# A state-space mixer and a mixture of experts on one core: row norms and weight splits ahead, the p projection moved into the router, one tile and one exponential per scan step

## The chip, the cores and the metric

The kernel runs on one core of a Trainium2 chip. The metric is the device time of one execution in microseconds (us). The engines are TensorE (PE, with its weight loads PEld), VectorE (DVE), ScalarE (ACT), GpSimd (POOL) and SyncE (SP), which here only issues transfers (DMA). Each engine works through its own queue in order and waits for others by semaphores.

## The reference

One layer on x (1024 tokens by 1024) with a side input p (1024 by 256), all float32:

```python
h = x + ssd_mixer(rms_norm(x), ...)        # in-projection, conv of 4 taps, chunked scan, out-projection
h = h + hier_moe(rms_norm(h), ...)         # 64 experts: best of 8 groups, then 2 of its 8 experts
gate = sigmoid(rms_norm(h) @ ple_w_gate + ple_b_gate)
h = h + gate * (p @ ple_w_proj)
out = rms_norm(h)
# the chunked scan, per chunk of 128 tokens and head, acum = cumsum(dt * A):
y_diag = (C B^T * tril(exp(acum[l] - acum[s]))) @ xc
y_off = C @ state * exp(acum)
state = state * exp(acum[-1]) + B^T (xc * exp(acum[-1] - acum))
```

## The kernel before

The work has three stages, one behind the other on PE.

**Scan stage (`ssd`).** The tokens are done in two halves (`hf`) of 512, and in each half four groups `g` of eight heads: eight units. For a half, `x_half` loads the rows of x to get their norms (squares on ACT or DVE, `rsqrt` on DVE), spreads the norms by four transposes on PE (line 177) into a tile along the tokens, loads the columns of x (`xT`), scales them and splits them into a high and a low part, `xh` and `xl`. A unit's `project` makes ten tiles of 128 channels: each loads 128 columns of `w_in`, splits them (`wh` on ACT, `wl` on DVE, line 70) and runs 24 matmuls (lines 204 to 206). Conv and SiLU follow on DVE and ACT. Between the ten tiles of a unit the scan of the unit before is placed by a plan of steps: `front(c)` of chunk c prepares and `back(c)` multiplies, in the order front 0, front 1, back 0, front 2, back 1, front 3, back 2, back 3. A front loads the running sums `acd` of its eight heads, broadcast over the partitions, into the tile `ac` (line 322), takes the exponential into `ec` (338), subtracts each token's own sum from `ac` in place (340), and takes the second exponential of that (342). The back's matmuls (369, 371) read both. `ac` has three buffers, which the row loads of x use too, and `ec` two. `step_sizes` writes `acd` once per half.

**Out-projection and router (`out_router`, `route`).** Eight token tiles in sets of 2, 3 and 3 go through 16 k steps (lines 505 to 507). The router's steps of a set (`stats`, `turn`, `logits`, `first`, `second`, `third`) run between the products of the next; those of the last set stand alone at the end: transposes (612), logits (618), positions (685 to 690), and two packings (714) from which the first gather of rows starts. Meanwhile `moe_weights` loads what the last stage needs.

**Expert stage (`moe`).** Eight groups of eight experts, in a manual order on PE. A group has 24 parts of 16 matmul instructions (line 1027), each on two weight tiles of 1 MB from a ring of eight (line 782). Between the parts stand other pieces: `spread` (1017), `combine` (1090, 1091), and, in the first half of a group, the gated side input of the group before (`ple`): transposes of h (898), 16 gate matmuls (908), and the projection of p: `fetch_p` gathers 128 rows of p, `turn_p` transposes them (855) and `project_p` multiplies them by `wpp` (861), whose result DVE takes from PSUM. Group 6 does two projections more, for the end (`early`).

Instructions whose place nothing fixes are put in order when the program is built, by the tile scheduler.

Of the kernel before, what the change touches and what calls it, by code (L numbers as in the profile page):

```python
# [20 lines left out]
KD = D // 128  # L21
# [20 lines left out]
class K:  # L42
# [64 lines left out]
    def ssd(self, left, right):  # L107
# [35 lines left out]
        def x_half(hf):  # L143

            ss, rs, *tmp = (wk.tile([128, HC], F32, name=n) for n in ("rs", "rs", "nt0", "nt1", "nt2"))
            cols = []

            def columns():
                for j in range(2):
                    w = wraw.tile([128, KD, 256], F32, name="w").rearrange("p a b -> p (a b)")  # L150
                    w = w.rearrange("p (k t) -> p k t", t=HT)
                    nc.sync.dma_start(w, a["xT"].rearrange("(k p) t -> p k t", p=128)[:, 4 * j:4 * j + 4,
                                                                                      hf * HT:(hf + 1) * HT])
                    cols.extend(w[:, k] for k in range(4))

            for i in range(HC):
                t = hf * HC + i
                xt = (wk.tile([128, D], F32, name="ec") if i == 3 else wk.tile([128, D], F32, name="ac", bufs=3))
                nc.sync.dma_start(xt, a["x"][t * 128:(t + 1) * 128, :])
                if i == HC - 1:  # L160
                    if hf == 0:
                        W.append(load(2 * DI, 2 * DI + 512))
                    columns()
# [14 lines left out]
            rsb = wk.tile([128, HT], F32, name="dT", bufs=1)  # L178
            nc.scalar.activation(rsb, pr.rearrange("p c t -> p (c t)"), AF.Copy)

            def scale(k):
                nc.vector.tensor_mul(cols[k], cols[k], rsb)
# [4 lines left out]
            yield  # L187
# [75 lines left out]
        def proj(w, i, x):  # L263
            wh = wsp.tile([128, KD, 128], F32R, name="wh")
            wl = wsp.tile([128, KD, 128], F32R, name="wl")
            self.split(wh, wl, w[:, :, i * 128:(i + 1) * 128])
            ps = self.ps_mm.tile([128, 512], F32, name="mm")
            mm3(ps, wh, wl, x)
            return ps

        def conv_tile(hf, w, i, x, m):
# [5 lines left out]
            ps = proj(w, i, x)  # L277
# [11 lines left out]
        def project(hf, g):  # L289
            x = X[hf]  # L290
            w = W.pop() if W else load(2 * DI + g * 128, 2 * DI + 512 + g * 128)
            xT, zT = [], zp.tile([128, 4, HT], F32, name="z")
            bT = conv_tile(hf, w, 0, x, 16 + g)
            yield
            cT = conv_tile(hf, w, 1, x, 20 + g)
            U[hf, g] = bT, cT, xT, zT
            yield
            for j in range(2):
                w = load(DI + g * 512 + j * 256)
                for i in range(2):  # L300
                    xT.append(conv_tile(hf, w, i, x, 4 * g + 2 * j + i))
                    yield
            for j in range(2):
                w = load(g * 512 + j * 256)
                for i in range(2):
                    nc.scalar.activation(zT[:, 2 * j + i], proj(w, i, x), AF.Silu)
                    yield

        def scan(hf, g):
# [6 lines left out]
            def front(c):  # L316
# [4 lines left out]
                ac = wk.tile([128, 8, Q], F32, name="ac", bufs=3)  # L321
                nc.sync.dma_start(ac, bass.AP(tensor=acd.tensor, offset=acd[8 * g:8 * g + 1, cg * Q:cg * Q + 1].offset,
# [89 lines left out]
        X, SZ, U, W = {}, {}, {}, []  # L412
        for i, _ in enumerate(x_half(0)):
            if i == 0:
                nc.sync.dma_start(gk, a["ssd_norm_kp"])
            if i == HC - 1:
                small_loads()
# [3 lines left out]
        for hf, g in units:  # L421
# [5 lines left out]
            if g == 0:  # L427
                for t in (0, 1, 7, 8):
                    at(t, next, sizes, None)
            if before:  # L430
                at(0, before[2])
                at(2, before[3])
# [5 lines left out]
            if hf == 0 and g == NG - 1:  # L438
                xg = x_half(1)
                for t in (3, 4, 5, 6, 7):  # L440
                    at(t, next, xg)
# [15 lines left out]
    def out_router(self, st, tail, after_tail):  # L457
# [18 lines left out]
        self.gdd = dp.tile([128, 8, NE], F32, name="gdd")  # L476
        macc = self.macc
# [82 lines left out]
        for f in side:  # L560
            f()
# [21 lines left out]
    def route(self, t0, hs, rp, pr_p, wr, rb, macc):  # L583
# [95 lines left out]
        def third():  # L679
# [3 lines left out]
            for i in range(n + 1):  # L683
# [5 lines left out]
                if t0:  # L689
                    nc.tensor.matmul(pa[:, i], lhsT=self.onesb, rhs=macc, start=False, stop=True)  # L690
            adj, was = tl("adj", 8)[:, 0], self.more
# [29 lines left out]
            pack(self.mid, omi)  # L721
            started = tc.issue_after(self.index(rp).ins) if t0 + n == T // 128 else nullcontext()
# [16 lines left out]
    def moe_weights(self, st):  # L739
# [3 lines left out]
        wpp = cp.tile([128, 2, D], F32, name="wpp")  # L743
# [4 lines left out]
        self.pl = (wpg, wpp, bg, fn, mgp)  # L748

        def loads():  # L750
# [6 lines left out]
            for k in range(2):  # L757
                nc.sync.dma_start(wpp[:, k], a["ple_w_proj"][k * 128:(k + 1) * 128])
                yield
# [3 lines left out]
            for _ in range(10):  # L763
# [30 lines left out]
    def moe_buffers(self, st, ring):  # L794
# [4 lines left out]
        self.p0, self.po = (hp.tile([128, PD], F32, name=f"p{i}") for i in range(2))  # L799
# [39 lines left out]
    def fetch_p(self, g):  # L839
        if g < NGR - 1:  # L840
            self.gather(self.p0, self.a["p"], g)
        if self.first_of(g + 1) or g == NGR - 1:
            self.gather(self.po, self.a["p"], NGR + SET[g])
# [8 lines left out]
    def turn_p(self, p, pT, pc_):  # L852
        pt = pc_.tile([128, 2, 128], F32, name="pc")
        for k in range(2):
            self.nc.tensor.transpose(pt[:, k], p[:, k * 128:(k + 1) * 128], self.ident)
        self.nc.scalar.activation(pT, pt, AF.Copy)

    def project_p(self, pT, hf, pc_):
        pq = pc_.tile([128, 512], F32, name="pc")
        for k in range(2):  # L860
            self.nc.tensor.matmul(pq, lhsT=pT[:, k], rhs=self.pl[1][:, k, hf * 512:hf * 512 + 512],  # L861
                                  start=(k == 0), stop=(k == 1))
        return pq

    def ple(self, h, p, store, wk, pq_, pc_, own=(), pr=None):
# [3 lines left out]
        wpg, wpp, bg, fn, mgp = self.pl  # L869
# [23 lines left out]
        def tr(k0):  # L893
# [6 lines left out]
            if k0 and pr is None:  # L900
                self.turn_p(p, new("pT", [128, 2, 128]), pc_)
# [26 lines left out]
    def moe(self, s2, ring, sa):  # L928
        nc, tc, a = self.nc, self.tc, self.a
        mgp = self.pl[4]  # L930
# [5 lines left out]
        part = {"vT": vx[:, 0:1024].rearrange("p (k t) -> p k t", k=KD), "gt": vx[:, 1024:1536],  # L936
                "pT": vx[:, 1536:1792].rearrange("p (k t) -> p k t", k=2)}
# [164 lines left out]
        def ple_of(G, i, own=part):  # L1102
# [3 lines left out]
                bounds_check=T - 1, oob_is_err=False), wk, ps1, ps2, own,  # L1106
                            None if i else G.pr)

        def project(p, o):

            self.turn_p(p, part["pT"], ps2)
            for hf in range(2):
# [346 lines left out]
```

## Time and profile before

| | us |
|---|---|
| median of 3 runs | 1950.36 (1946.88 to 1954.07) |
| the profiled execution | 1954.31 |
| its span, first to last instruction | 1952.4 |
| PE busy in the span | 1848.3 |

The page's first part gives the busy time of each engine, the second its share in 40 equal slices with the granted clock of TensorE, the third the transfers; the chain of waits follows the work back from its end, and the groups of instructions name line, tile and mean duration. The lines are those of the kernel before.

### The profile page before, as it was taken

The numbers are of one execution on the slowest core, as the hardware profiler recorded it, in microseconds if no ns is written. First come the engines' busy times: TensorE is split into PE (matmuls) and PEld (weight loads), VectorE is DVE, ScalarE is ACT, GpSimd is POOL, SyncE is SP. The second block draws the span as 40 slices with busy tenths as digits, with TensorE's granted clock in tenths as the row PEclk, the third lists the DMA queues.
The fourth block names the chain that finished last, engine by engine and source line by source line (L and its number), as shares of the span: only waits on it lengthen the run. The fifth ranks groups of instructions, "written<-read, shape, count | busy, mean of one in ns | idle before, by whom it ended". The sixth has DMA issues, their size and how long they took to land.

```text
span 1952.4 us, 23158 instructions
## 1 busy us (share of the span) xinstructions
PE 1848.3 (95%) x8702; PEld 1047.1 (54%) x8702; DVE 1031.5 (53%) x2194; ACT 749.5 (38%) x1040; POOL 182.7 (9%) x276
## 2 busy tenths in 40 slices
PE   6999997999999999979999999999999999999996
PEld 4778775777887678863343333433433334334334
DVE  5497896858988876573341514423325244143223
ACT  5476766557767533322021211312222113122223
POOL 1011110201111031021000000000000000000004
PEclk9999998999999999988999999999999999999998
DMA  7425444345442787956999999999999999998883
GB/s 220 118 75 137 115 134 127 88 97 134 110 110 53 243 294 238 346 195 254 422 421 394 401 421 385 412 412 383 420 382 404 420 373 423 404 375 325 337 322 109
DMA packets 192166, 538.39 MB, mean 276 GB/s; under 512 B 16046, under 2 KB 128688, under 8 KB 143920
## 3 DMA queue, kind: packets, MB, share of 16 engines
q1 hardware_dynamic: 177744, 514.21, 72.0%
q10 hardware_dynamic: 11008, 12.94, 2.0%
q0 software_dynamic: 3296, 9.70, 1.3%
q8 instruction: 70, 1.15, 0.2%
q14 instruction: 48, 0.39, 0.1%
HBM read 520.95 MB, written 17.69 MB: 276 GB/s over the span
## 4 chain that ended last, share of the span: by engine, by line
PE 81%; DMA 7%; DVE 7%; ACT 2%; issue 2%; POOL 1%; SPq 0%; POOLq 0%; ACTq 0%; DVEq 0%
PE pup L1027 11%; PE pgate L1027 11%; PE py L1027 10%; PE mm L206 6%; PE mm L204 6%; PE mm L205 6%; PE pq L908 6%; PE pc L1017 3%; PE mm L505 2%; PE mm L506 2%; PE mm L507 2%; DMA w<-in_w_up_dram 2%; PE pc L861 2%; DMA ac<-acd 2%; PE pc L1090 2%
## 5 line engine op out<-in xcount | busy, mean ns | idle before, releaser
L204 PE MATMUL mm<-xh,wh 128*128 128x512 f32 x640 | 265.6, 415 | 3.3 <-ACT xh L197 2.2
L206 PE MATMUL mm<-xh,wl 128*128 128x512 f32 x640 | 254.5, 400 | 8.4 <-DVE wl L70 8.3
L205 PE MATMUL mm<-xl,wh 128*128 128x512 f32 x640 | 253.9, 397 | 0.3 <-DVE xl L198 0.3
L1027 PE MATMUL pup<-w,XT 128*64 128x512 f32 x1016 | 239.1, 598 | 1.6 <-DMA w<-in_w_up_dram 1.6
L1027 PE MATMUL pgate<-w,XT 128*64 128x512 f32 x1000 | 232.7, 599 | 0.0
L1027 PE MATMUL py<-w,hT 128*64 128x512 f32 (+1 forms) x1024 | 227.1, 586 | 2.1 <-DMA w<-in_w_down_dram 2.1
L70 DVE TENSOR_TENSOR yx<-py,yx 128x512 fp32r<-128x512 f32 (+1 forms) x68 | 44.8, 659 | 234.2 <-ACT yx L69 234.2
L1027 PEld LDWEIGHTS py<-w,hT 128*64 128x64 f32 x1024 | 70.0, 137 | 146.2 <-issue 138.2
L1027 PEld LDWEIGHTS pup<-w,XT 128*64 128x64 f32 x1016 | 72.1, 136 | 141.9 <-issue 131.5
L206 PEld LDWEIGHTS mm<-xh,wl 128*128 128x128 f32 x640 | 122.6, 192 | 38.5 <-DVE wl L70 12.2
L204 PEld LDWEIGHTS mm<-xh,wh 128*128 128x128 f32 x640 | 122.9, 192 | 34.2 <-issue 4.5
L1027 PEld LDWEIGHTS pgate<-w,XT 128*64 128x64 f32 x1000 | 68.7, 137 | 134.2 <-issue 129.6
L205 PEld LDWEIGHTS mm<-xl,wh 128*128 128x128 f32 x640 | 123.0, 192 | 29.9 <-issue 4.3
L908 PE MATMUL pq<-wpg,vx 128*128 128x512 f32 x256 | 123.1, 607 | 0.0
L70 DVE TENSOR_TENSOR wl<-w,wh 128x1024 fp32r<-128x1024 f32 x80 | 97.4, 1220 | 46.4 <-ACT wh L69 46.4
L69 ACT ACTIVATE wh<-w 128x1024 fp32r<-128x1024 f32 x80 | 84.3, 1054 | 72.0 <-PE mm L205 59.4
L284 DVE SCALAR_TENSOR_TENSOR xbc<-raw,convw,xbc 128x512 f32<-128x512 f32 x144 | 109.7, 762 | 3.8 <-ACT xbc L282 2.7
L506 PE MATMUL mm<-wl,yh 128*128 128x512 f32 x256 | 99.3, 398 | 2.0 <-DVE wl L517 1.9
L505 PE MATMUL mm<-wh,yh 128*128 128x512 f32 x256 | 96.0, 402 | 4.8 <-ACT yh L69 4.6
L69 ACT ACTIVATE yx<-py 128x512 fp32r<-128x512 f32 (+1 forms) x68 | 38.9, 572 | 159.4 <-PE py L1027 159.4
L1058 ACT ACTIVATE hT<-pt 128x512 f32<-128x512 f32 x31 | 18.4, 593 | 211.5 <-PE pt L1056 211.5
L507 PE MATMUL mm<-wh,yl 128*128 128x512 f32 x256 | 98.0, 393 | 0.0
(360 smaller groups left out, 2815.6 us busy)
## 6 DMA issues: line engine op xcount, KB each, us to landing
w<-in_w_up_dram SPq DMA_DIRECT2D x127, 1024.0 KB, 9.5
w<-in_w_gate_dram SPq DMA_DIRECT2D x125, 1024.0 KB, 9.1
w<-in_w_down_dram SPq DMA_DIRECT2D x120, 1024.0 KB, 9.5
w<-in_w_in_dram SPq DMA_DIRECT2D x32, 1024.0 KB, 5.6
w<-in_w_out_dram SPq DMA_DIRECT2D x48, 512.0 KB, 5.2
ac<-acd SPq DMA_DIRECT2D x32, 512.0 KB, 9.3
w<-in_w_in_dram SPq DMA_DIRECT2D x16, 512.0 KB, 8.7
yn<-yz SPq DMA_DIRECT2D x32, 256.0 KB, 4.4
```

The lines of the kernel that those rows point to most:

```text
L69: self.nc.scalar.activation(dst_h, src, AF.Copy)
L70: self.nc.vector.tensor_sub(dst_l, src, r_(dst_h))
L204: nc.tensor.matmul(ps, lhsT=wh[:, k], rhs=x[0][:, k], start=(k == 0), stop=False)
L205: nc.tensor.matmul(ps, lhsT=wh[:, k], rhs=x[1][:, k], start=False, stop=False)
L206: nc.tensor.matmul(ps, lhsT=wl[:, k], rhs=x[0][:, k], start=False, stop=(k == KD - 1))
L284: nc.vector.scalar_tensor_tensor(o, raw[:, j:j + HT], convw[:, m, j:j + 1], o, op0=OP.mult, op1=OP.add)
L505: nc.tensor.matmul(po[i][hf], lhsT=yh[:, ts], rhs=wh[:, cs], start=(k == 0), stop=False)
L506: nc.tensor.matmul(po[i][hf], lhsT=yh[:, ts], rhs=wl[:, cs], start=False, stop=False)
L507: nc.tensor.matmul(po[i][hf], lhsT=yl[:, ts], rhs=wh[:, cs], start=False, stop=(k == 15))
L908: nc.tensor.matmul(V["pq"], lhsT=V["vT"][:, k], rhs=wpg[:, k, cs], start=(k == 0), stop=(k == KD - 1))
L1017: nc.tensor.matmul(px, lhsT=x[:, k], rhs=G.S[:, i], start=(i == 0 and x is u[i][0]), stop=(i == 1 and x is u[i][1]))
L1027: nc.tensor.matmul(ps[64 * b:64 * b + 64], lhsT=xt(k0 + k, b), rhs=w[b][:, k, cs], start=(k0 + k == 0), stop=(k0 + k == K - 1))
```

## The change

Five edits. (1) The row norms are a piece of work of their own, `norms(hf)`; those of the second half run in the first unit, and their result has a tile of its own, `rsb`. (2) The splits of `w_in` come from one generator, and each tile's split is asked for before the tile ahead of it has been finished. (3) A front's sums and differences lie in one tile `ae` with two buffers; the load goes to its first half, the subtraction writes the second, and one exponential covers both. The steps `norm` and `store` of a unit stand one step later in the plan. (4) p is handed over transposed and projected for all tokens in the router's last steps, in 16 pieces of two matmuls; the result goes to memory as `ppd`. (5) The expert stage gathers rows of `ppd` (1024 wide) in place of rows of p (256 wide), five steps later, and transposes and multiplies nothing for it.

```diff
+            pr = self.ps_tp.tile([128, HC, 128], F32, name="tp")
...
+            RB[hf] = wk.tile([128, HT], F32, name="rsb", bufs=1)
+            nc.scalar.activation(RB[hf], pr.rearrange("p c t -> p (c t)"), AF.Copy)
+            yield
...
+        def proj(x):
+
+            wh, wl = ahead.pop() if ahead else next(W)
             ps = self.ps_mm.tile([128, 512], F32, name="mm")
             mm3(ps, wh, wl, x)
+            ahead.extend(w for w in [next(W, None)] if w)
             return ps
...
-                ac = wk.tile([128, 8, Q], F32, name="ac", bufs=3)
-                nc.sync.dma_start(ac, bass.AP(tensor=acd.tensor, offset=acd[8 * g:8 * g + 1, cg * Q:cg * Q + 1].offset,
+                ae = wk.tile([128, 2, 8, Q], F32, name="ae")
+                ec, ac = ae[:, 0], ae[:, 1]
+                nc.sync.dma_start(ec, bass.AP(tensor=acd.tensor, offset=acd[8 * g:8 * g + 1, cg * Q:cg * Q + 1].offset,
...
-                ec = wk.tile([128, 8, Q], F32, name="ec")
-                nc.scalar.activation(ec, ac, AF.Exp)
                 for h in range(8):
-                    nc.vector.tensor_scalar(ac[:, h], ac[:, h], acs[:, c, 8 * g + h:8 * g + h + 1], 0.0,
+                    nc.vector.tensor_scalar(ac[:, h], ec[:, h], acs[:, c, 8 * g + h:8 * g + h + 1], 0.0,
                                             op0=OP.subtract, op1=OP.min)
-                nc.scalar.activation(ac, ac, AF.Exp)
+                nc.scalar.activation(ae, ae, AF.Exp)
...
+                if hf == 0:
+                    rows = norms(1)
+                    for t in (2, 3, 4, 5, 6):
+                        at(t, next, rows)
...
+        def project():
+
+            for t in range(T // 128):
+                pr = wp.tile([128, D], F32, name="wl")
+                for hf in range(2):
+                    cs = slice(hf * 512, hf * 512 + 512)
+                    pq = self.ps_mm.tile([128, 512], F32, name="mm")
+                    for k in range(2):
+                        nc.tensor.matmul(pq, lhsT=pT[k][:, t * 128:(t + 1) * 128], rhs=wpp[k][:, cs],
+                                         start=(k == 0), stop=(k == 1))
+                    nc.scalar.activation(pr[:, cs], pq, AF.Copy)
+                    if hf:
+                        nc.sync.dma_start(self.ppd[t * 128:(t + 1) * 128], pr)
+                    yield
...
+            for n, f in zip((6, 0, 0), side[-3:]):
+                f() if f is not side[-1] else f(lambda n: [next(pieces, None) for _ in range(n)])
+                for _ in range(n):
+                    next(pieces)
+            for _ in pieces:
+                pass
...
-            if k0 and pr is None:
-                self.turn_p(p, new("pT", [128, 2, 128]), pc_)
...
-            nc.vector.tensor_mul(gt, gt, self.project_p(V["pT"], hf, pc_) if pr is None else pr[:, cs])
+            nc.vector.tensor_mul(gt, gt, pr[:, cs])
...
-                    fill[2].append(lambda: self.gather(vx[:, 1792:], a["p"], g + 1))
-                    early = [project(vx[:, 1792:], nxt.pr), project(self.p0, cur.pr)]
...
-                    if n == 10:
+                    if n == 15:
                         self.fetch_p(g)
```

Three places in the order of the built programs follow. The first is on PE. Before, the transposes that spread the second half's norms (`tp<-ident,rs`) stand inside the group of 24 matmuls that begins the second half:

```order
L205 MATMUL mm<-xl,wh 128x512
L206 MATMUL mm<-xh,wl 128x512
L204 MATMUL mm<-xh,wh 128x512
L177 MATMUL tp<-ident,rs 128x128 x4
L205 MATMUL mm<-xl,wh 128x512
L206 MATMUL mm<-xh,wl 128x512
```

Now they stand between two tiles of the very first unit:

```order
L205 MATMUL mm<-xl,wh 128x512
L206 MATMUL mm<-xh,wl 128x512
L165 MATMUL tp<-ident,rs 128x128 x4
L204 MATMUL mm<-xh,wh 128x512
L205 MATMUL mm<-xl,wh 128x512
L206 MATMUL mm<-xh,wl 128x512
```

So the row norms of the second half, with their loads, are past long before its first matmul.

The second is on SP, behind the write of the sums `acd` in the second unit; `w` are weight tiles of `w_in`. Before:

```order
L253 DMA acd<-dT 32x512
L322 DMA ac<-acd 128x8x128 x3
L260 DMA w<-in_w_in_dram 128x8x256
L322 DMA ac<-acd 128x8x128
L260 DMA w<-in_w_in_dram 128x8x128 x2
L260 DMA w<-in_w_in_dram 128x8x256
L322 DMA ac<-acd 128x8x128 x2
```

Now:

```order
L253 DMA acd<-dT 32x512
L334 DMA ae<-acd 128x8x128 x2
L260 DMA w<-in_w_in_dram 128x8x256
L260 DMA w<-in_w_in_dram 128x8x128 x2
L334 DMA ae<-acd 128x8x128
L260 DMA w<-in_w_in_dram 128x8x256
L334 DMA ae<-acd 128x8x128
```

Two broadcasts instead of three go ahead, and from then on a broadcast and a weight load take turns.

The third is on PE, at the end of the router. Before, the logits of the last token tile (`tp<-wr,uT`) are followed at once by the positions (`tris`, `onesb`):

```order
L612 MATMUL tp<-ident,h 128x128 x8
L618 MATMUL tp<-wr,uT 128x72 x8
L688 LDWEIGHTS tris
L688 MATMUL tp<-M,tris 128x72
L690 LDWEIGHTS onesb
L690 MATMUL tp<-macc,onesb 128x72
```

Now six pieces of the projection (`mm<-w,wh`, twelve matmuls) stand between them:

```order
L660 MATMUL tp<-ident,h 128x128 x8
L666 MATMUL tp<-wr,uT 128x72 x8
L593 MATMUL mm<-w,wh 128x512 x12
L736 LDWEIGHTS tris
L736 MATMUL tp<-M,tris 128x72
L738 LDWEIGHTS onesb
L738 MATMUL tp<-macc,onesb 128x72
```

Two more pieces follow the positions, two the first packing, and the last six the second packing, ahead of the first `spread`.

## Rows read from the trace of the kernel before

**Rows 1.** The page, part 1: busy us of each engine (share of the span) and instructions.

```profile
PE 1848.3 (95%) x8702; PEld 1047.1 (54%) x8702; DVE 1031.5 (53%) x2194; ACT 749.5 (38%) x1040; POOL 182.7 (9%) x276
```

**Rows 2.** Busy time by stretch, all engines. Columns: stretch and its length, busy us of PE, PEld, DVE, ACT and POOL with the number of instructions, granted clock, busy share of the DMA engines, GB/s.

```profile
90.00:112.00 22.00, 17.19 (x73) 12.48 (x72) 15.63 (x36) 15.96 (x20) 1.78 (x5) 0.84 0.23 71
290.00:335.00 45.00, 31.48 (x150) 23.61 (x149) 28.41 (x81) 27.00 (x34) 3.03 (x4) 0.85 0.45 130
360.00:380.00 20.00, 15.31 (x79) 12.70 (x80) 18.88 (x39) 12.05 (x16) 4.12 (x7) 0.83 0.40 95
...
858.00:890.00 32.00, 17.75 (x94) 11.44 (x94) 22.87 (x87) 8.77 (x16) 9.92 (x19) 0.68 0.43 150
```

**Rows 3.** What PE waited for in the whole run (us in total, times, longest).

```profile
PE mm L206 <- DVE wl L70: 8.3, 8, 2.2
...
PE py L369 <- DVE ac L352: 3.6, 2, 3.5
...
PE py L1027 <- DMA w<-in_w_down_dram: 2.1, 2, 1.3
```

**Rows 4.** The same between 250 and 500 us.

```profile
PE tp L177 <- DVE rs L66: 7.8, 1, 7.8
```

**Rows 5.** Pieces of the chain of waits that are transfers in the scan stage (start, us, what).

```profile
80.56 12.30 DMA ac<-acd
286.85 10.97 DMA ec<-in_x_dram
309.70 9.82 DMA ac<-acd
```

**Rows 6.** The issues of the broadcast loads of the sums in the whole run (queue, count, KB each, median us from issue to landing).

```profile
ac<-acd SPq DMA_DIRECT2D x32, 512.0 KB, 9.3
```

**Rows 7.** The time to landing of all transfers that touch `acd`.

```profile
DMA to landing us min/median/max: 1.6/9.3/15.1
```

**Rows 8.** What SP's queue waited for in front of these issues (us in total, times, longest).

```profile
SPq L322 <- PE py L371: 132.1, 18, 16.9
```

**Rows 9.** Loads of ACT's function tables ahead of the two exponentials (groups of instructions: count, busy us, mean ns, idle before).

```profile
L342 ACT ACT_TABLE_LOAD x24 | 30.8, 1283 | 7.4 <-DVE ed L346 2.8 <-DMA rb<-in_b_re_dram 2.3 <-DVE ac L340 2.1
...
L338 ACT ACT_TABLE_LOAD x21 | 26.9, 1283 | 0.7 <-DMA ac<-acd 0.4
```

**Rows 10.** What DVE waited for at the subtraction in the whole run (us in total, times, longest).

```profile
DVE ac L340 <- ACT ec L338: 23.3, 7, 9.6
```

**Rows 11.** Two groups of DVE instructions, the subtraction and the low part of a split, in the whole run (duration ns, least, median, most; first and last start).

```profile
L340 DVE TENSOR_SCALAR ac<-ac,acs x256: 269/279/842, 89.1 to 676.2; 128x128 f32<-128x128 f32 x128
...
L70 DVE TENSOR_TENSOR wl<-w,wh x80: 1155/1218/1325, 12.7 to 624.4; 128x1024 fp32r<-128x1024 f32 x80
```

**Rows 12.** PE in the scan stage in order of time: the first and the last of fifteen matmuls in a row, with fourteen starts between them (start, duration us).

```profile
33.10 0.39 PE L204 MATMUL mm<-xh,wh 128*128 128x512 f32 x1
...
36.28 0.39 PE L206 MATMUL mm<-xh,wl 128*128 128x512 f32 x1
```

**Rows 13.** The projection of p on PE, all of it as one group of instructions (count, busy us, mean ns, idle before and what ended it).

```profile
L861 PE MATMUL pc<-wpp,vx 128*128 128x512 f32 x72 | 36.3, 627 | 5.0 <-ACT vx L856 2.5 <-DVE ha L1092 1.3 <-DVE hb L1092 1.3
```

**Rows 14.** One projection's pieces on PE in order of time (start, us).

```profile
1149.87 0.38 PE L855 MATMUL pc<-ident,p 128*128 128x128 f32 x2
1150.18 3.65 PE L1027 MATMUL pgate<-w,XT 128*64 128x512 f32 x16
...
1177.66 1.98 PE L861 MATMUL pc<-wpp,vx 128*128 128x512 f32 x4 [0.32 <-DVE hb L1092]
1179.57 3.65 PE L1027 MATMUL pup<-w,XT 128*64 128x512 f32 x16
```

**Rows 15.** The chain of waits at the same point (the first part of the last `down`) of groups 1, 5 and 6, that is at the start of the next group's work; between the first two lie four groups.

```profile
1120.99 3.58 PE py L1027 x16
...
1633.47 3.58 PE py L1027 x16
...
1773.72 3.58 PE py L1027 x16
```

**Rows 16.** Busy time by stretch in the expert stage, columns as in rows 2.

```profile
1100.00:1180.00 80.00, 79.03 (x332) 30.48 (x330) 24.96 (x46) 19.73 (x33) 2.03 (x2) 1.00 1.01 421
1180.00:1230.00 50.00, 50.00 (x208) 17.63 (x206) 19.73 (x40) 10.16 (x15) 2.12 (x2) 1.00 0.98 378
1230.00:1310.00 80.00, 79.03 (x332) 30.33 (x328) 25.39 (x46) 18.88 (x32) 1.28 (x2) 1.00 1.01 421
```

**Rows 17.** The issues of expert weights (count, KB each, median us to landing).

```profile
w<-in_w_up_dram SPq DMA_DIRECT2D x127, 1024.0 KB, 9.5
```

**Rows 18.** PE at the end of the router and the start of the expert stage, in order of time (in brackets the idle time before and what ended it).

```profile
862.39 2.00 PE L618 MATMUL tp<-wr,uT 128*128 128x72 f32 x16
868.82 0.22 PE L688 MATMUL tp<-M,tris 128*128 128x72 bf16 x1 [4.42 <-DVE me L664]
...
872.51 0.33 PE L714 MATMUL tp<-omi,at 128*128 128x16 bf16 x6 [2.76 <-DVE at L706]
874.27 0.70 PE L714 MATMUL tp<-oms,at 128*128 128x104 bf16 x6 [1.43 <-DVE oms L728]
879.77 1.22 PE L1017 MATMUL pc<-S,uh 128*128 128x512 f32 x2 [4.80 <-ACT uh L1003]
...
889.76 3.65 PE L1027 MATMUL pgate<-w,XT 128*64 128x512 f32 x14
```

More of the change, by code (lines that the diff above doesn't have):

```diff
@@ L141, in small_loads, with norms @@
             nc.sync.dma_start(al, bcast_rows(a["a_log"], 128, 0, NH))
-        def x_half(hf):
+        def norms(hf):
             ss, rs, *tmp = (wk.tile([128, HC], F32, name=n) for n in ("rs", "rs", "nt0", "nt1", "nt2"))
[L146 to L154, printed above, removed]
             for i in range(HC):
                 t = hf * HC + i
-                xt = (wk.tile([128, D], F32, name="ec") if i == 3 else wk.tile([128, D], F32, name="ac", bufs=3))
+                if i % 2 == 0:
+                    two = wk.tile([128, 2, D], F32, name="ae")
+                xt = two[:, i % 2]
                 nc.sync.dma_start(xt, a["x"][t * 128:(t + 1) * 128, :])
[L160 to L163, printed above, removed]
                 if hf == 0 and i % 2:
@@ L261, in load, with weights, conv_tile @@
             return w
[L263 to L266, printed above, removed]
+        def weights():
+            for hf in range(2):
+                for g in range(NG):
+                    for cols in ((2 * DI + g * 128, 2 * DI + 512 + g * 128), *((DI * a_ + g * 512 + j * 256,)
+                                                                               for a_ in (1, 0) for j in range(2))):
+                        w = load(*cols)
+                        for i in range(2):
+                            wh = wsp.tile([128, KD, 128], F32R, name="wh")
+                            wl = wsp.tile([128, KD, 128], F32R, name="wl")
+                            self.split(wh, wl, w[:, :, i * 128:(i + 1) * 128])
+                            yield wh, wl
+        W = weights()
+        ahead = []
+        def proj(x):
+            wh, wl = ahead.pop() if ahead else next(W)
             ps = self.ps_mm.tile([128, 512], F32, name="mm")
             mm3(ps, wh, wl, x)
+            ahead.extend(w for w in [next(W, None)] if w)
             return ps
[L271 removed]
+        def conv_tile(hf, x, m):
             raw = rawp.tile([128, 3 + HT], F32, name="raw")
@@ L410, in scan @@
             return front, back, norm, store
-        X, SZ, U, W = {}, {}, {}, []
-        for i, _ in enumerate(x_half(0)):
+        X, SZ, U, RB = {}, {}, {}, {}
+        first, xg = norms(0), x_half(0)
+        for i in range(HC):
+            next(first)
             if i == 0:
                 nc.sync.dma_start(gk, a["ssd_norm_kp"])
-            if i == HC - 1:
-                small_loads()
+        ahead.append(next(W))
+        next(xg)
+        small_loads()
+        next(first)
+        next(xg)
         sizes = step_sizes(0)
@@ L476, in out_router @@
         self.gdd = dp.tile([128, 8, NE], F32, name="gdd")
+        self.ppd = dp.tile([T, D], F32, name="ppd")
         macc = self.macc
@@ L762, in loads @@
             nc.sync.dma_start(fn, bcast_rows(a["final_norm"], 128, 0, D))
-            for _ in range(10):
+            for _ in range(12):
                 yield
@@ L850, in parts, with ple @@
         mm(to, lhsT=v[1][:, k], rhs=w[0], start=False, stop=(k == KD - 1))
[L852 to L865, printed above, removed]
+    def ple(self, h, pr, store, wk, pq_, pc_, own=()):
         nc = self.nc
-        wpg, wpp, bg, fn, mgp = self.pl
+        wpg, bg, fn, mgp = self.pl
         V = dict(own)
@@ L1281, in moe @@
                 if g == NGR - 2:
-                    nxt.pr, cur.pr = self.h0[(g + 2) % 3], self.ho[(SET[g] - 1) % 3]
-                    fill[2].append(lambda: self.gather(vx[:, 1792:], a["p"], g + 1))
-                    early = [project(vx[:, 1792:], nxt.pr), project(self.p0, cur.pr)]
-                    for n, x in ((17, 0), (18, 0), (20, 1), (21, 1)):
-                        fill.setdefault(n, []).append(lambda x=x: next(early[x]))
+                    nxt.pr = self.h0[(g + 2) % 3]
+                    fill.setdefault(17, []).append(lambda: self.gather(nxt.pr, self.ppd, g + 1))
                 if nxt:
```

96 lines of the change are left out of this document (49 added, 47 removed).

## The prediction

> **What bounds the kernel now.** I read the busy times first: PE works 95% of the span, ACT 38%, DVE 53% [rows 1]. So the time is PE's work plus what PE loses: idle time, and time at a lower granted clock. Second, the windows by stretch: in three places of the scan and at the router's end PE idles and the clock lies at 0.68 to 0.85 of the higher of its two levels, 2.4 GHz [rows 2]; in the expert stage it is 1.00. Third, PE's waits by releaser, for the causes: the low part `wl` of a split (8.3 us in 8 waits) and the back's tile `ac` (3.6) in the scan, expert weights for only 2.1 [rows 3], and one wait of 7.8 us for the norms of the second half [rows 4]. Fourth, the chain of waits, which turns to transfers at just these places of the scan: the broadcast of the sums (12.30 and 9.82 us) and the load of x's rows (10.97) [rows 5].
>
> All sums below are made against the profiled execution, 1954.31 us. The median of the runs is 4 us lower, and the forecast is moved by as much at the end. What a measurement of this kernel can tell from no change is 0.5%, or 10 us.
>
> **Norms of the second half ahead.** The four transposes stand inside the first group of matmuls of the second half, and PE is in order: it stops there until the rows of x have landed and the norms are out. The stretch of 45 us holds 31.48 us of PE work [rows 2]: 13.5 us idle, and 45 × 0.15 = 6.75 us by which the clock fell short. All of it gone is 20.3; the wait alone is 7.8. The transposes themselves remain, and the row loads move to the first unit, where the DMA engines were 23% busy in the stretch read [rows 2]. What is late next is the scaling and splitting of x's columns on DVE, 28.41 us busy in those 45, so not all of the gap goes. I take −17 (bounds −7.8 to −20.3).
>
> **Splits a tile ahead, backs a tile later.** This aims at the waits for `wl` and `ac`, 8.3 + 3.6 us [rows 3]. They sit in stretches such as 90 to 112 (4.8 us idle, 3.5 by the clock) and 360 to 380 (4.7 and 3.4), 16.4 together [rows 2]. A split that is asked for a tile early has a tile of PE time more, but stands in DVE's queue behind other work all the same. I take −9, three quarters of the waits, between nothing and the 16.4 of the two stretches.
>
> **One tile and one exponential.** The order of the built program holds 96 loads of ACT's function tables in place of 128: 32 × 1.283 = 41 us of ACT [rows 9]. ACT is off the path, so I count nothing for it by itself. DVE's wait of 23.3 us for the first exponential [rows 10] goes too; DVE now waits for the transfer itself. What is new is that the tile has two buffers for three: the broadcasts of chunks 2 and 3 can go out only when the backs 0 and 1 have read theirs. SP waited for backs before as well, 132.1 us in 18 waits [rows 8], but with one chunk more of lead. The matmuls come every (36.28 − 33.10) / 14 = 0.227 us [rows 12], a tile of 24 takes 5.5. After a back come two tiles, 11.0 us, with the transposes of a front, and then the next back, an estimated 4 us: 15 in all until PE needs the split that stands behind the subtractions on DVE. A broadcast lands after 9.3 us at the median [rows 6], the eight subtractions take 8 × 0.28 and the split 1.2 [rows 11]: 12.7, some 2 us to spare. The longest landing is 15.1 [rows 7]. Of 14 such chunks (two in each of seven scans that run beside tiles) half land later than the median, on average halfway to the longest, at 12.2: 0.9 over the margin, 6.3 us in all. I take +6. The bounds are wide: −10, if DVE without its 23.3 us of waiting gives PE half of that, and +57, if every one of the 14 landed at 15.1 with no more cover than the two tiles.
>
> The scan's net is −17 − 9 + 6 = −20.
>
> **What leaves the expert stage.** A projection of p costs PE two pieces of 1179.57 − 1177.66 = 1.91 us and its transposes 1150.18 − 1149.87 = 0.31 [rows 14]: 4.13. The 72 records [rows 13] are nine projections of four matmuls, each recorded twice: groups 1 to 5 hold one each, group 6 three, group 7 one. From the chain a group's period is (1633.47 − 1120.99) / 4 = 128.1 us, and group 6 takes 140.25 [rows 15]. Without the projection PE's own time is 128.1 − 4.2 = 123.9 (0.1 of idle time with it).
>
> The transfers then come close. A group loads 24 × 2 weight tiles of 1024 KB (1.0486 MB) [rows 17], 50.33 MB; the gathers of h and the output are 0.52 MB each, and the gather of p grows from 0.13 to 0.52: 51.9 MB. At 421 GB/s, which the busiest stretches reach with a busy share of 1.01 [rows 16], that is 123.3 us. PE's 123.9 and the DMA's 123.3 so near each other will not fit without gaps: I take 125.0 per group, 3.1 × 5 = 15.5. Group 6 drops its three projections (12.4) but not below its transfers: 125.5, a gain of 14.7. Group 7 gives 4.1. Together −34, at most 9 × 4.2 + 4 = −42 with the idle time at those places, at least −16 (below, rival A). DVE loses transposes' copies and takes the product from memory instead of PSUM, which it has time for (24.96 of 80 us busy [rows 16]). POOL's gather moves from step 10 to 15, its rows are four times as wide, and the first use is at the next group.
>
> On the rate the trace and the notes differ. The trace shows 421 GB/s with one core at work [rows 16]. The Trainium skill (DMA: Bandwidth & Descriptors, "Where 436 GB/s comes from") puts a ceiling of about 435 GB/s on the DMA fabric and says that transfers between HBM and SBUF are bound by the HBM side, near 358 GB/s. By 358 a group's 51.9 MB would take 145 us, more than the 128.1 that a group takes now, and by 435 it would take 119.3; the trace disagrees with the first.
>
> **What comes into the router.** 16 pieces of 1.91 us are 30.6 us of PE work. The end of the router has holes: 32 − 17.75 = 14.25 us idle from 858 to 890, at a clock of 0.68, 10 us short [rows 2]. Before, the logits end at 864.4, positions begin at 868.82, and 889.76 is the first `pgate` [rows 18]. Now six pieces (11.5) stand ahead of the positions: 875.9, +7.1. Two pieces (3.8) stand in the 3.7 us from there to the packing of 872.51, of which 0.7 is PE's other work there: +0.8. Two fill the one before 874.27 (1.76): +2.4 more at most. The last six (11.5) lie over the gather of rows and the 4.80 us that PE waited there. 862.39 + 2.00, sixteen pieces and the positions and packings (0.22, 0.33, 0.70) make 896.3, and the spread's 16 matmuls behind it at an estimated 4.5 us give 901 in place of 889.76. So +11. Bounds: +6 (the clock stays up, and the chains on DVE hide under the pieces) and +30.6. On SP the eight writes of `ppd` stand in front of three weight loads, which go out some 30 us later than at 860; PE needs those tiles after 901, and the DMA engines were 43% busy there [rows 2], so I count nothing; without that cover one load costs its 9.5 us [rows 17].
>
> **Sum:** −20 − 34 + 11 = −43, or 1911 us for the profiled execution, 1907 for the median.
>
> **Rivals.**
> A. The weight stream already bounds the expert stage. For it: share 1.01 and 421 GB/s [rows 16], and four times the bytes for p. Against it: PE waits for weights only 2.1 us [rows 3]. Groups 1 to 5 would then give nothing, groups 6 and 7 some 16 us, as they have more PE work than transfers: −20 + 11 − 16 = −25, at 1925.
> B, slower: the two buffers. The broadcast covers only one tile, because the front's work on DVE holds up the next split from the moment the load is issued: each of the 14 chunks waits 9.3 − 5.5 = 3.8 us at the median landing, and 6.8 at the chain's 12.30 [rows 5]. At 5.3, halfway, the 14 are 74 us in place of the +6: −43 + 68 = +25, at 1975. It decides for slower from (43 + 6 + 10) / 14 = 4.2 us per chunk. For it: SP's waits of 132.1 [rows 8] and landings to 15.1 [rows 7]. Against it: two full tiles stand there in the order.
> C. Everything hides: the scan runs without waits (−40 with its clock), the expert stage gives 40 and the router takes 11: −69, at 1881. For it: PE is the bound in both stages, and idle time costs clock too. Against it: the DMA's 123.3.
> The change also would not do what it says if the scheduler put the transposes back next to their first use; the order shows that it doesn't.
>
> **How the numbers follow.** The forecast has a chance of 0.71, with a range of its own of 1892 to 1922 (scan −30 to −10, router +6 to +18, experts −40 to −26, not all at one end). A has 0.12, C 0.10, B 0.07. The range for 8 in 10 is 1884 to 1934: it takes in A, and most of the way to C and a mild B. Faster by over 0.5% means below 1940: forecast, A and C, less a little for the router's and the scan's upper bounds coming together: 0.90. B gives slower 0.07, between lies 0.03.
>
> **What would show it.** Right: no wait of PE for `rs` near 290; the waits for `wl` gone; 96 table loads; 125 us from group to group, 126 in group 6, with a few us of waits for expert weights on PE; some 32 us from the end of the logits to the first matmul of the spread (15.4 before). Wrong for (A): a period of 128 and long waits for `w` on PE. Wrong for (B): DVE waiting for `ae` from memory and behind it PE for `wl`, with a clock under 0.9 across the scan. The forecast falls if the scan comes out longer than before, or if the router adds more than 20 us.

## The result, and the profile after

Slower by 1%: 1969.55 us (median of 4, 1966.55 to 1975.06) against 1950.2 of before on the same chip, a ratio of 1.0102 with a 95% interval of 1.0069 to 1.0134. Forecast were 1907 us, and faster.

Where the time went is read from three lines in each trace, each giving the first and last start of one kind of matmul: the scan's tiles, the router's logits, the first expert product. Before:

```profile
L204 PE MATMUL mm<-xh,wh x640: 387/389/798, 17.8 to 633.0; 128*128 128x512 f32 x160
...
L618 PE MATMUL tp<-wr,uT x128: 225/275/330, 719.9 to 864.1; 128*128 128x72 f32 x128
...
L1027 PE MATMUL pgate<-w,XT x1000: 592/592/1117, 886.7 to 1892.8; 128*64 128x512 f32 x167
```

After:

```profile
L204 PE MATMUL mm<-xh,wh x640: 387/389/798, 18.9 to 646.0; 128*128 128x512 f32 x160
...
L666 PE MATMUL tp<-wr,uT x128: 223/275/330, 752.3 to 896.2; 128*128 128x72 f32 x128
...
L1057 PE MATMUL pgate<-w,XT x1000: 592/592/644, 932.1 to 1904.4; 128*64 128x512 f32 x167
```

The scan ends 13.0 us later, the logits 32.1, so the out-projection, in which the last unit's scan runs, is 19.1 longer. The router's end goes from 22.6 to 35.9 us, +13.3. From the first `pgate` to the last it is 1006.1 before and 972.3 after, −33.8. The last two are close to the forecast (+11 and −34); the loss lies ahead of them. Over the work up to the last logits, from 60 us on, it is idle time of PE in the main (columns as in [rows 2]; the first line is before, the second after):

```profile
60.00:864.00 804.00, 763.82 (x4153) 609.03 (x4152) 619.04 (x1347) 474.89 (x592) 112.49 (x180) 0.98 0.53 155
...
60.00:896.00 836.00, 774.12 (x4158) 615.62 (x4156) 609.96 (x1333) 422.41 (x520) 109.20 (x179) 0.96 0.50 146
```

PE idles 40.2 us of the first and 61.9 of the second, 21.7 more; the other 10.3 are busy time, at a granted clock of 0.96 for 0.98.

The expert stage's groups begin with the same matmul (PE in order of time):

```profile
1159.10 0.50 PE L1047 MATMUL pc<-S,uh 128*128 128x512 f32 x1 [0.62 <-DVE hb L1122]
...
1659.19 0.49 PE L1047 MATMUL pc<-S,uh 128*128 128x512 f32 x1 [0.62 <-DVE hb L1122]
...
1784.80 0.50 PE L1047 MATMUL pc<-S,uh 128*128 128x512 f32 x1 [0.62 <-DVE ha L1122]
```

Four groups lie between the first two, 125.0 us each, and group 6 takes 125.6; 125.0 and 125.5 were forecast. PE waits for expert weights 5.2 us, the part for `w_down` as before [rows 3]:

```profile
PE pup L1057 <- DMA w<-in_w_up_dram: 3.1, 5, 0.9
...
PE py L1057 <- DMA w<-in_w_down_dram: 2.1, 2, 1.3
```

At the router's end (compare [rows 18]) PE hardly idles any more: from the last logits to the spread it projects p (29.32 of the 31 us from 896 to 927 are busy), and the granted clock is 1.00 there, where it was 0.68 from 858 to 890 [rows 2]:

```profile
894.45 2.00 PE L666 MATMUL tp<-wr,uT 128*128 128x72 f32 x16
896.29 10.51 PE L593 MATMUL mm<-w,wh 128*128 128x512 f32 x24
...
914.52 8.81 PE L593 MATMUL mm<-w,wh 128*128 128x512 f32 x20
924.06 1.98 PE L593 MATMUL mm<-w,wh 128*128 128x512 f32 x4 [0.73 <-ACT wl L595]
927.01 0.74 PE L1047 MATMUL pc<-S,uh 128*128 128x512 f32 x2 [0.96 <-DVE S L1000]
```

Now the scan. What the engines waited for there in the changed kernel (us in total, times, longest):

```profile
DVE ae L350 <- DMA ae<-acd: 83.1, 22, 8.4
...
PE tp L341 <- DVE yz L415: 12.5, 4, 4.0
PE mm L204 <- ACT wh L69: 11.6, 3, 5.2
PE mm L526 <- DVE wl L537: 10.0, 6, 5.6
PE mm L206 <- DVE wl L70: 9.6, 8, 2.5
```

DVE stands 83.1 us at the subtraction, for the broadcast itself; before, it stood there 23.3, for the exponential [rows 10]. PE's waits name other tiles, splits and stores, not the broadcast. One place shows the link. Broadcast, DVE, ACT and PE in order of time, at the start of the last unit:

```profile
556.69 0.36 SPq L334 DMA_DIRECT2D ae<-acd  x1
...
565.94 1.66 DVE L350 TENSOR_SCALAR ae<-ae,acs 128x128 f32<-128x128 f32 x8 [5.16 <-DMA ae<-acd]
...
567.67 1.28 ACT L352 ACT_TABLE_LOAD   x1 [6.13 <-DVE ae L350]
568.96 1.91 ACT L352 ACTIVATE ae<-ae 128x2048 f32<-128x2048 f32 x1
570.89 1.28 ACT L317 ACT_TABLE_LOAD   x1
...
572.67 1.05 ACT L69 ACTIVATE wh<-w 128x1024 fp32r<-128x1024 f32 x1
...
573.75 1.23 DVE L70 TENSOR_TENSOR wl<-w,wh 128x1024 fp32r<-128x1024 f32 x1 [1.42 <-ACT wh L69]
...
573.77 0.79 PE L204 MATMUL mm<-xh,wh 128*128 128x512 f32 x1 [5.23 <-ACT wh L69]
```

The broadcast goes out at 556.69 and the subtraction can start at 565.94. DVE has been idle for 5.16 us; ACT, whose next instruction is the exponential of both halves, for 6.13; behind that stands the split's high part, and behind it the low part and PE. This front is chunk 1 of its scan. The clock in the stretch around it falls too (columns as in [rows 2]):

```profile
560.00:580.00 20.00, 14.73 (x57) 11.45 (x56) 10.05 (x21) 9.41 (x11) 1.56 (x3) 0.83 0.34 74
```

### The profile page after: what moved, and what is told of

It is laid out like the page before. It is cut to its first block, busy times and chain, and to the rows that moved or that the text cites. A ratio compares the mean times of both kernels' runs of the same rounds, so it can differ in the third digit from the quotient of the medians.

```text
span 1965.0 us, 23067 instructions
## 1 busy us (share of the span) xinstructions
PE 1846.2 (94%) x8676; PEld 1053.1 (54%) x8676; DVE 1024.9 (52%) x2194; ACT 704.5 (36%) x979; POOL 176.6 (9%) x276
## 5 line engine op out<-in xcount | busy, mean ns | idle before, releaser
L204 PE MATMUL mm<-xh,wh 128*128 128x512 f32 x640 | 270.0, 422 | 14.2 <-ACT wh L69 11.6
L206 PE MATMUL mm<-xh,wl 128*128 128x512 f32 x640 | 258.9, 405 | 9.7 <-DVE wl L70 9.6
L1057 PE MATMUL pup<-w,XT 128*64 128x512 f32 x1016 | 243.4, 598 | 3.3 <-DMA w<-in_w_up_dram 3.1
L1057 PEld LDWEIGHTS pup<-w,XT 128*64 128x64 f32 x1016 | 77.5, 136 | 139.5 <-issue 120.5
L939 PE MATMUL pq<-wpg,vx 128*128 128x512 f32 x256 | 123.2, 607 | 0.0
L70 DVE TENSOR_TENSOR wl<-w,wh 128x1024 fp32r<-128x1024 f32 x80 | 97.6, 1220 | 23.3 <-ACT wh L69 23.1
L350 DVE TENSOR_SCALAR ae<-ae,acs 128x128 f32<-128x128 f32 x256 | 60.3, 304 | 83.2 <-DMA ae<-acd 83.1
```

The source lines that it names most:

```text
L70: self.nc.vector.tensor_sub(dst_l, src, r_(dst_h))
L204: nc.tensor.matmul(ps, lhsT=wh[:, k], rhs=x[0][:, k], start=(k == 0), stop=False)
L206: nc.tensor.matmul(ps, lhsT=wl[:, k], rhs=x[0][:, k], start=False, stop=(k == KD - 1))
L350: nc.vector.tensor_scalar(ac[:, h], ec[:, h], acs[:, c, 8 * g + h:8 * g + h + 1], 0.0, op0=OP.subtract, op1=OP.min)
L939: nc.tensor.matmul(V["pq"], lhsT=V["vT"][:, k], rhs=wpg[:, k, cs], start=(k == 0), stop=(k == KD - 1))
L1057: nc.tensor.matmul(ps[64 * b:64 * b + 64], lhsT=xt(k0 + k, b), rhs=w[b][:, k, cs], start=(k0 + k == 0), stop=(k0 + k == K - 1))
```

## The experiments

Two theories. The two buffers: a broadcast can go out only when the back two chunks earlier has read its tile. Its rival, the place: in the joint tile the subtraction needs only the landing, not an exponential first, so it stands early in DVE's queue, and the exponential behind it holds ACT. A third: not the tile, but the other edits of the scan. All ratios are to the kernel before on the same chip. Two runs on different chips are compared by their ratios; the difference is given in us of the kernel before.

**The halves of the change alone.** The scan functions of one kernel with the rest of the other.

```diff
- scan of after, router and expert stage of after
+ e1: scan of before, router and expert stage of after
+ e2: scan of after, router and expert stage of before
```

> The scan of before with edits 4 and 5 (p projected in the router). If the parts add up, this takes before's time, plus the 13 us by which the router's end grew, less the 34 us that the expert stage gained: about 1930 us, and logits end at 864 as before. If the loads of p's operands in front of the out-projection's end cost part of the 19 us that the out-projection grew by, it comes out at 1935 to 1949.

Measured 1939.47 us, 0.9929 [0.9902, 0.9957]: logits end 2.8 us later than before, router's end +13.1, expert stage −30.2.

> Edits 1 to 3 alone, on the router and expert stage of before. If all the loss is in the scan and what of it runs beside the out-projection, the time is before's plus 13 plus 19: about 1982 us. If the out-projection's 19 us belong to edit 4, about 1963 us.

Measured 1987.9 us, 1.0170 [1.0145, 1.0196]. Scan end +15.7 and out-projection +22 are all there without edits 4 and 5. The two changes add up to the changed kernel's (−0.7% + 1.7% = +1.0%): the loss belongs to edits 1 to 3.

**The tile undone (e3), then undone with two buffers (e4: the same without `bufs=3`).**

```diff
-                ae = wk.tile([128, 2, 8, Q], F32, name="ae")
+                ac = wk.tile([128, 8, Q], F32, name="ac", bufs=3)
...
+                ec = wk.tile([128, 8, Q], F32, name="ec")
+                nc.scalar.activation(ec, ac, AF.Exp)
```

> The changed kernel with edit 3's tile undone: sums in three buffers of their own, two exponentials, the first before the subtraction; norms and splits ahead and the later steps stay. If the tile (two buffers, one exponential) is the cause, the gain of the transition (16 us) stays and the losses of units 2, 3 and 7 (28 us) and most of the out-projection's 19 go: 1925 to 1935 us. If the splits ahead or the later steps are the cause, it stays at 1962 to 1972 us.

Measured 1920.47 us, 0.9829 [0.9803, 0.9855], 5 us under the range and 2.7%, or 53 us, under the changed kernel: the tile is the cause.

> As the run before, but the tile of the sums has two buffers, so that a broadcast goes out as late as in the changed kernel, while ACT takes two exponentials in the old order. If the late issue is what costs, this is like the changed kernel, 1960 to 1972 us, with DVE or ACT waiting some 80 us for the broadcast to land. If it is that one exponential waits for the subtraction and holds ACT's splits behind it, it is like the run before, 1925 to 1940 us.

Measured 2031.45 us, 1.0404 [1.0376, 1.0432], far above all that was expected. Here the first exponential waits for the landing, so it is ACT that stands:

```profile
ACT ec L347 <- DMA ac<-acd: 90.7, 18, 7.6
ACT L347 <- DMA ac<-acd: 67.6, 12, 9.0
```

It shows that two buffers can cost much, not that they do in the joint tile. They also moved the order: ACT comes to the first exponential 8.4 us after the issue of the broadcast at the median, where it was 17.4 in e3.

**Three buffers for the joint tile.**

```diff
-                ae = wk.tile([128, 2, 8, Q], F32, name="ae")
+                ae = wk.tile([128, 2, 8, Q], F32, name="ae", bufs=3)
...
-                yz = wk.tile([128, 4, Q], F32, name="yz", bufs=6)
+                yz = wk.tile([128, 4, Q], F32, name="yz", bufs=5)
...
-            sqs = wk.tile([128, HC, Q], F32, name="sqs")
+            sqs = wk.tile([128, HC, Q], F32, name="sqs", bufs=1)
```

> The changed kernel with three buffers for the joint tile in place of two (room for it: one buffer of the gated outputs fewer, five for six, and one in place of two for the sums of squares). If the buffers alone made the loss, this is at the level of the separate tiles, 1912 to 1926 us, and the wait of DVE for broadcasts falls from 83 us to some 20. If the one exponential behind the subtraction costs as well, it is 1930 to 1950 us.

Measured 1958.7 us, 1.0022 [1.0003, 1.0042]: above both expectations. The third buffer takes 0.8%, or 16 us, off the changed kernel, and most of the loss is left. DVE's wait is as long as with two:

```profile
DVE ae L350 <- DMA ae<-acd: 81.3, 23, 7.9
```

So the theory of the two buffers alone falls. (With three buffers the subtraction came as early after its broadcast as with two; the table of these lags is below.)

**The other edits, undone one at a time on the separate tiles (1920 us).**

```diff
- e6: norms(1) at steps 2 to 6 of the first unit
+ e6: norms(1) at steps 3 to 7 of the fourth, x_half(1) at its step 8
- e7: ahead.extend(w for w in [next(W, None)] if w)
- e8: at(1, before[2]), at(3, before[3])
+ e8: at(0, before[2]), at(2, before[3])
```

> The separate tiles again (1920 us), with the row norms of the second half asked for in the last unit of the first, as before the change. If the transition gained what its gap showed, PE waits for the norms again and the time is up by 12 to 20 us, 1932 to 1940. If that gap is filled by something else by now, no change.

> The separate tiles again, with each split asked for at its own tile. If the splits ahead gained the 9 us of the forecast, 1926 to 1934 us with waits of PE for the low part back; if they gain nothing, 1917 to 1924; if they hold up the weight loads on SP and so cost, below 1917.

> The separate tiles again, with the steps that take a unit's norm and store at their old places (0 and 2 for 1 and 3). If the later places collide with the fronts, as PE's waits of 12.5 us for the stores in the changed kernel let one think, below 1916; if those waits were only the tail of the late broadcasts, 1917 to 1924.

Measured e6 1922.9 us (0.9846 [0.9818, 0.9874]), e7 1940.46 (0.9924 [0.9900, 0.9948]), e8 1921.55 (0.9838 [0.9807, 0.9869]). e7 lies above all of its ranges. The steps do nothing that can be measured. With e1 and e3, which have neither and both, e6 and e7 make a square: neither 0.9929, norms ahead 0.9924, splits ahead 0.9846, both 0.9829. The splits ahead gain 16 to 19 us, the norms ahead nothing that can be measured.

**A tile later in the program.** The subtraction, exponential and products become a function `rest`, called a step after the load.

```diff
-                for t, f, c in ((0, front, 0), (1, front, 1), (2, back, 0), (3, front, 2), (4, back, 1),
+                for t, f, c in ((0, front, 0), (1, rest, 0), (1, front, 1), (2, rest, 1), (2, back, 0), (3, front, 2),
+                                (4, rest, 2), (4, back, 1), (5, front, 3), (6, rest, 3), (6, back, 2), (8, back, 3)):
```

> The changed kernel, joint tile with two buffers, but a front is cut in two: the load and the transposes at its old step, the subtraction, exponential and what follows one tile later (chunk c at steps 1, 2, 4 and 6 of a unit). If what costs is that the subtractions stand on DVE right behind the issue of a broadcast that takes 9 us, a tile of 5.5 to 7 us more lead takes most of DVE's wait of 83 us away, and the time comes to 1915 to 1935 us. If two buffers cost by themselves (the late issue), the wait moves on to the back's matmuls on PE and the time stays at 1955 to 1975.

> The same cut with three buffers of the joint tile (with five gated outputs and one buffer for the sums of squares): 1905 to 1925 us if lead on DVE decides, with a wait of DVE for the broadcasts under 25 us; 1950 to 1965, as with three buffers and no cut, if the cut does nothing.

> The same cut on the two separate tiles (1920 us), both exponentials a tile later. DVE's wait there is 36 us and ACT's 22; if these still cost, 1900 to 1916 us; if the backs then wait for the exponentials, 1920 to 1935.

Measured e9 1983.08 us (1.0155 [1.0129, 1.0180]), e10 1951.23 (0.9985 [0.9970, 1.0000]), e11 1917.76 (0.9814 [0.9793, 0.9834]). A miss for e9 and e10; e11 is no different from e3. The line of e9 says why:

```profile
DVE ae L359 <- DMA ae<-acd: 81.4, 20, 8.1
```

The same wait. A step later in the program is not later in DVE's queue, since the tile scheduler sets that order: DVE comes to the subtraction 5.9 us after the issue at the median, where it was 6.2 in the changed kernel. So the place itself had not been tried yet. The third buffer is worth more here, 1.7% from e9 to e10.

**The place held by an order edge.** The subtractions stand on DVE behind the low part of the latest split (`low` is that instruction): e12 is the changed kernel with this edge and nothing else, e13 the three buffers of e5 with it, e14 e10 with it, e15 e11 with it.

```diff
+                with tc.issue_after(low[0].ins):
-                for h in range(8):
+                    for h in range(8):
```

In the order of the built programs on DVE, at the end of the third unit's work, the first front's subtraction comes one split later: in the trace of the changed kernel `stc<-st,ed` (230.25 us) and one low part (231.54) stand ahead of it, with the edge the same `stc` and two. The changed kernel, its last three groups:

```
L70 TENSOR_TENSOR wl<-w,wh 128x1024
L350 TENSOR_SCALAR ae<-ae,acs 128x128 x8
L356 COPY ed<-ae 128x8
```

With the edge:

```
L70 TENSOR_TENSOR wl<-w,wh 128x1024
L377 TENSOR_TENSOR stc_113<-st,ed 128x512
L70 TENSOR_TENSOR wl<-w,wh 128x1024
L394 SCALAR_TENSOR_TENSOR yz<-xbc,dsk,py 128x128 x3
L388 TENSOR_TENSOR stc_113<-stc_113,pst 128x512
L394 SCALAR_TENSOR_TENSOR yz<-xbc,dsk,py 128x128
L396 TENSOR_TENSOR yz<-yz,z 128x512
L70 TENSOR_TENSOR wl<-w,wh 128x1024
L352 TENSOR_SCALAR ae<-ae,acs 128x128 x8
```

> The changed kernel, joint tile with two buffers, with one order edge: a front's subtractions stand on DVE behind the low part of the split that was asked for last. If it is their place on DVE that costs, the time falls by 15 us or more, to 1925 to 1955; if the late issue of the broadcasts by two buffers is what decides, it stays within 1960 to 1980.

> The same order edge with three buffers of the joint tile (five gated outputs, one buffer for the sums of squares); where read, DVE's order is the same as in the run before, so the two differ by the issue of the broadcasts alone. If place and buffers both count, this is where the loss is gone: 1912 to 1928 us, DVE's wait for the broadcasts under 30 us. If the joint exponential itself costs, 1935 to 1955.

> Three buffers, the order edge, and the subtraction a tile later in the program: 1905 to 1922 us if more lead still helps, above the run before if the backs then wait for the exponential on PE.

> The two separate tiles, a tile later (1918 us) with the order edge on the subtractions: 1905 to 1917 us if DVE's 36 us of waiting for the first exponential still hold up splits, no change or up to 10 us more if they don't.

Measured e12 1916.39 us (0.9820 [0.9801, 0.9838]), e13 1909.66 (0.9787 [0.9764, 0.9810]), e14 1909.07 (0.9775 [0.9755, 0.9796]), e15 1930.17 (0.9884 [0.9864, 0.9904]). e12 and e13 come out below their ranges, e15 above. One edge, with the two buffers and the one exponential left as they are, takes 2.8%, or 55 us, off the changed kernel. In e12 DVE's waits have changed places: the broadcast is nearly gone, and what DVE stands at longest in the scan is the split itself, for its high part (60 to 760 us; 19.9 us in the changed kernel).

```profile
DVE wl L70 <- ACT wh L69: 55.9, 17, 4.7
...
DVE ae L352 <- DMA ae<-acd: 16.7, 4, 5.9
```

DVE at the start of the last unit, in order of time (chunk 0 of the scan, one front ahead of the one shown for the changed kernel; neither front is waited for here):

```profile
532.87 1.23 DVE L70 TENSOR_TENSOR wl<-w,wh 128x1024 fp32r<-128x1024 f32 x1 [4.59 <-ACT wh L69]
534.01 1.65 DVE L352 TENSOR_SCALAR ae<-ae,acs 128x128 f32<-128x128 f32 x8
```

The stretch around it, columns as in [rows 2]:

```profile
520.00:540.00 20.00, 20.00 (x115) 16.49 (x114) 9.34 (x22) 10.24 (x14) 2.43 (x4) 1.00 0.63 189
```

The low part now goes first, the subtractions find their data landed, and PE works through the stretch at a clock of 1.00 (14.73 of 20 us at 0.83 above). From 60 us to the last logits (847) PE idles 22.3 us, where it was 61.9 in the changed kernel. The third buffer is worth another 6 us, and DVE's wait with it is

```profile
DVE ae L352 <- DMA ae<-acd: 7.9, 3, 3.6
```

More lead beyond that (e14) gives nothing, and on the separate tiles (e15) the edge does harm, 0.7% over e11. DVE's wait for the first exponential only changes places there (35.5 us at the subtraction in e11, 36.2 at the copy `ed` in e15), so it does not explain the harm; its cause is open. e13 and e14 are the fastest versions run, 42 to 44 us under before.

**The place in all of these runs.** The lag from the issue of a broadcast to the moment at which DVE comes to its subtraction (the start of the first of the eight, less DVE's idle time before it), at the median of the 32 fronts; a broadcast lands after 8.4 to 9.6 us at the median in these runs:

| run | tiles and buffers | lag, us | ratio to before |
|---|---|---|---|
| before | separate, 3 | 21.4 | 1 |
| changed kernel | joint, 2 | 6.2 | 1.0102 |
| e3 | separate, 3 | 20.4 | 0.9829 |
| e4 | separate, 2 | 7.9 | 1.0404 |
| e5 | joint, 3 | 6.8 | 1.0022 |
| e9, e10 | joint, 2 and 3, a step later | 5.9, 6.0 | 1.0155, 0.9985 |
| e11 | separate, 3, a step later | 20.1 | 0.9814 |
| e12, e13 | joint, 2 and 3, with the edge | 14.3, 31.5 | 0.9820, 0.9787 |
| e14 | joint, 3, a step later, with the edge | 34.5 | 0.9775 |
| e15 | separate, 3, a step later, with the edge | 36.2 | 0.9884 |

Below the row of before, the versions with a lag under the landing are at 0.9985 or above, and those with a lag over it at 0.9884 or below. The edge lets the scheduler place other instructions anew as well; which of them moved was read on DVE alone.

## Why the prediction was wrong

**One tile and one exponential** is the step that failed. It gave +6 us; measured are +53 (from e3, 0.9829, to 1.0102) and +55 (from e12, 0.9820). It set a landing after 9.3 us, the subtractions and the split, 12.7 in all, against 15 us until PE needs the split, "some 2 us to spare", and it did so for chunks 2 and 3 alone.

The landing it had right (9.1 at the median). Three other parts of the sum were wrong.

- *What was counted.* DVE stood on the transfer 22 times in 32 fronts, 83.1 us. Of these, 14 times and 54.8 us fall on chunks 0 and 1, which the step put at nothing. Their broadcasts need the buffers of chunks 2 and 3 of the scan before.
- *The cover.* In the place shown, a chunk 1, PE stops at 568.54 (573.77 − 5.23), 11.9 us after the issue: two tiles and a front's transposes, and no back. The back that the step added, estimated at 4 us, would have taken 3.1 (283.73 to 286.81 in the trace of before).
- *The chain.* The split's low part stands behind its high part, and that stood on ACT behind the exponential and another activation, with a table load before each (1.28). The high part ends at 573.72, 17.0 us after the issue and not 12.7. The step did not price ACT, which has to hold its in-order place until DVE has subtracted (6.13 us).

Behind all three stands the place: the step asked when PE needs the split, not when DVE comes to the subtraction. DVE comes early, 6.2 us after the issue, where it was 21.4 before. The step had named the cover that went (DVE's 23.3 us for the exponential) as a gain; with the exponential in front of it the subtraction stood late, in before and in e3. That +53 lies near the upper bound of +57 is luck: the bound set 15.1 − 11.0 = 4.1 us against each of the 14 chunks and left out the subtractions and the split that the step's own sum has; with them it is 7.5 each, 106 us.

Rival B had the chain right, with DVE held and the next split behind it, and put 1975 us to it; it had 0.07. Its cause, the two buffers, decides 6 us when the place is right, and 16 (e5) to 33 (e10 against e9) when it is not. Of its sign, DVE waits for `ae` as it said, but the clock is 0.96 across the scan (60 to 646 us), not under 0.9. Its threshold was for the forecast's other terms: 53 to 55 over 14 chunks is 3.8 to 3.9 each, under 4.2, and the kernel came out slower all the same because the others gave less.

**Norms ahead**, −17: the wait for `rs` near 290 is gone as expected, and from the start of tile 8 of the fourth unit to tile 1 of the next (counted from 0) it takes 31.2 us in e7 where before took 45.4 and e1 43.4. But e1 and e7 end alike: at the start of the fifth unit e7 is 8.9 us ahead of e1, at that of the last 1.8. The gain is given back in the units behind; by what was not tried. With the splits ahead the stretch is 24.4 us even with late norms (e6): so the gap was not the norms' alone, for which the step had taken it. Its bound of −20.3 also set the clock's shortfall against idle time; on the 31.48 us busy it is 4.7, and the bound 18.2.

**Splits ahead**, −9: too small, 16 to 19 by the square, and only in part by the mechanism named. Of the two waits it aimed at, that for `ac` went (3.6 us in e1 and e7, none in e6 and e3), but PE's waits for `wl` in the in-projection stayed: 9.9 us in e1 and 7.6 in e6, 4.3 in e7 and 5.6 in e3. PE's idle time up to the last logits as a whole falls, from 60.4 to 48.8 us and from 56.5 to 48.3; what else made it fall was not traced.

**Expert stage**, −34: −33.8, at 125.0 us a group, and rival A falls (a period of 128 would have shown it). In e1 it was −30.2. PE is busy 123.2 us of a group, where 123.9 was worked out, and idle 1.8; that the step put 1.1 us of gaps on top was a guess that fitted. In group 6 its 14.7 is 2.3 more than the 12.4 us of projections that leave, without a reason given, and 125.6 was measured for its 125.5. **Router**, +11: +13.3 by the first `pgate`, and from the end of the logits to the spread 30.6 us (927.01 − 894.45 − 2.00) for 32. **The whole**: e1's −0.7% and e2's +1.7% make up the +1.0% that was measured. By way of e1 and e3 it is −14 us for the p projection, −20 for norms and splits, and +53 for the tile.

The rate of the transfers stayed at 421 GB/s at the best (1180 to 1230 us) with a share of 1.01, as in [rows 16].

## What to carry to other kernels

Taking a step out in front of an instruction also takes away what kept that instruction late: on an in-order engine, ask where it will stand in the queue and whether its transfer has landed by then, and read that from the order against a measured landing (here 6.2 us against 9.1). A wait of an engine that is half idle is not free when the next thing in its queue feeds the engine that bounds the kernel. If the order is set by a scheduler, moving a call in the program may move nothing; an order edge does.
